# Activation sides in three stages, down slabs by column pairs, and state space copies on GpSimd's queue, in a decoder layer on one core

## The chip, the cores and the metric

The kernel runs on one core of a Trainium2 chip. A core has five engines, each with its own queue of instructions that it works off in order: TensorE (PE, matrix products), VectorE (DVE), ScalarE (ACT), GpSimd (POOL) and SyncE (SP, which here only starts transfers). They wait for each other by semaphores. Transfers between memory and SBUF are started by an instruction on some engine's queue and then run by themselves. The metric is the time of one execution on the device in microseconds (us), as the median of several runs.

## The reference

One decoder layer, for 512 tokens of width 1024, in float32:

```python
Layer = x + 1/2 SwiGLU(RMSNorm x)                       (macaron first half-step)
      -> x + W_out[ sig(g_nsa) * Y_nsa + sig(g_ssm) * Y_ssm ]   (parallel gated token mixers)
      -> x + 1/2 SwiGLU(RMSNorm x)                       (macaron second half-step)

def _rmsnorm(x, g):
    return xf * lax.rsqrt(jnp.mean(xf * xf, axis=-1, keepdims=True) + RMS_EPS) * g
def _swiglu(x, g, w_gate, w_up, w_down):
    h = _rmsnorm(x, g)
    return (jax.nn.silu(h @ w_gate) * (h @ w_up)) @ w_down
```

The hidden width of both feed-forward halves is 2816, which is 22 tiles of 128 (f tiles). Y_nsa is an attention with compressed, selected and windowed keys; Y_ssm is an S5 state space: u is projected from x, runs through a complex diagonal recurrence in time, gets a GELU and a gated linear unit.

## The kernel before, in words

Data lies transposed, features on the 128 partitions and the 512 tokens along the row. Every large product is made as three matmuls (`mm3`, L372): a float32 operand is split into a hi part (a copy rounded by ACT) and a lo part (the rest, by DVE), and hi x hi, lo x hi and hi x lo are added up in PSUM. Weights arrive as slabs of 128x1024 floats, which are eight blocks of 128x128. SP starts the transfers in the order of the plan (`wraw`, four buffers), ACT makes `whi` (L235), DVE `wlo` (L236), three buffers each, two slabs ahead of TensorE. A slab of eight blocks is 24 matmuls of 128x512.

TensorE's instructions stand in the order of the program; on the other engines a scheduler sets the order from the order of emission, priorities and dependencies, so what waits on an engine is also waited for by all that stands behind it there.

The second feed-forward half (`fast_ffn`, L481 on) has two parts. The first four f tiles are plain: gate and up, eight k blocks each. The other 18 are taken in nine pairs, gate and up of both tiles as a 2x2 block product by seven half-size products instead of eight (P1 to P7). Each product (`product`, L542) is 24 matmuls of 128x256. Their weight operands are sums of the four weight quarters, added up on DVE (L260) in `wpair` buffers (transfers of 512 KB) and then split like any slab. Their activation operands ("sides") are sums of the normalised x tiles k and k+4, in halves of 256 tokens: `side(k)` (L490) makes all seven for one k of four, on DVE, with hi copies `xqh` on ACT (L507) and `xql` on DVE (L508). `side(0)` to `side(2)` are emitted after plain tiles 1 to 3, the last one after tile 3 too. The results go to banks mA, mB and mC: P1, P6, P7 and P4 add up in mA, and ACT copies mA to SBUF after P1, P6 and P7 (`mP`, L563).

The down projection is added in five chunks (4 f tiles, then pairs 2, 2, 2, 3), as slabs of eight blocks that stand between products (`DOWN_AT`). A chunk's slabs can begin when its f tiles have their activation split into `ah` and `al` (L518, L519). `down` (L587) keeps one PSUM bank per output column that is begun; when a column has all f tiles of the chunk, DVE adds it to the residual (`xd`, read from `xhome`) and GpSimd's queue writes it back (L607), or in the last chunk SP stores the output.

The norm of the second half is made from `nacc` (sums of squares, GpSimd, L396); `norm.a` and `norm.b` (from L400) make the row factor `R` with small matmuls on TensorE.

In the state space part, `u_evac` (L977) writes a tile of u to DRAM and reads it back in another layout (one write of 256 KB, four reads of 64 KB); `s5_out` (L1081) does the same with the GELU's result in hi and lo halves: `gd` writes, `gT` reads. All of these are issued on the queue named `DU`, which is SP's. `s5m`, `str` and `sti` are the state's scratch tiles, `qh` and `ql` the query projection's parts, `kt` a transposed key.

Of the kernel before, what the change touches and what calls it, by code (L numbers as in the profile page):

```python
# [46 lines left out]

HEAD = 4
PAIR_CHUNKS = [2, 2, 2, 3]
DOWN_AT = [(1, 1), (1, 1), (1, 1), (1, 1), (1, 1), (1, 1), (1, 1), (1, 0), (1, 0)]  # L50


def fast_steps():

    np_ = (FF // 128 - HEAD) // 2
    ends = [HEAD]
    for n in PAIR_CHUNKS:
        ends.append(ends[-1] + 2 * n)
    down = []
    for c, e in enumerate(ends):  # L60
        b = ends[c - 1] if c else 0
        blocks = [(c, d, f) for d in range(KD) for f in range(b, e)]
        down.append([blocks[i:i + 8] for i in range(0, len(blocks), 8)])
    queue = []
    steps = [("plain", f) for f in range(HEAD)] + [("prod", 0, "P1")]
    nxt, done = 0, 0
    queue += down[0]
    for i in range(np_):
        a, b = DOWN_AT[i]
        steps += [("prod", i, "P2"), ("prod", i, "P6")]  # L70
        steps += [("down", queue.pop(0)) for _ in range(min(a, len(queue)))]
        steps += [("prod", i, "P5"), ("prod", i, "P7")]
        if i + 1 < np_:
            steps.append(("prod", i + 1, "P1"))
        steps += [("down", queue.pop(0)) for _ in range(min(b, len(queue)))]
        steps += [("prod", i, "P4"), ("prod", i, "P3")]
        done += 1
        if done == PAIR_CHUNKS[nxt]:
            assert not queue
            nxt, done = nxt + 1, 0  # L80
            queue += down[nxt]
    return steps + [("down", q) for q in queue], ends


# [210 lines left out]

def build(ctx, tc, xT_in, wstream, small_in, out):
    nc = tc.nc
    DU, DQ, DX = nc.sync, nc.sync, nc.sync
    V, S, G, PE = nc.vector, nc.scalar, nc.gpsimd, nc.tensor
    ctx.enter_context(tc.manual_schedule(engines={mybir.EngineType.PE}))  # L300
    cp = ctx.enter_context(tc.tile_pool(name="const", bufs=1))
# [5 lines left out]
    def H(name, dt=F32):  # L307
        return hp.tile([128, 512], dt, name=name, tag="h", bufs=NH)
# [25 lines left out]
    def smc(n, a=0, b=None):  # L334
        s, e = SM[n]
        return sm[:, s + a:(s + b if b is not None else e)]
# [144 lines left out]
    def fast_ffn(p, gname, x, norm, xgh, xgl, home, nxt):  # L481

        steps, ends = fast_steps()
        X = {}
        act, pss, left = {}, {}, {}
        bank, cq, ut = {}, {}, {}
        ng = cp.tile([128, KD], F32, name=f"ng_{p}")
        V.tensor_scalar(ng, smc(gname), -1.0, None, op0=ALU.mult)

        def side(k):  # L490

            R = norm.R
            a, b = slice(0, 256), slice(256, 512)
            ga, na, gb, nb = (t[:, i:i + 1] for i in (k, k + 4) for t in (smc(gname), ng))
            q1, q2, q3, q4 = (H(f"xq{i}") for i in range(4))
            V.scalar_tensor_tensor(q1[:, a], x[k][:, a], na, R[:, a], op0=ALU.mult, op1=ALU.mult)
            V.scalar_tensor_tensor(q4[:, b], x[k][:, b], ga, R[:, b], op0=ALU.mult, op1=ALU.mult)
            V.scalar_tensor_tensor(q2[:, a], x[k + 4][:, a], gb, R[:, a], op0=ALU.mult, op1=ALU.mult)
            V.scalar_tensor_tensor(q3[:, a], x[k + 4][:, b], nb, R[:, b], op0=ALU.mult, op1=ALU.mult)
            x[k] = x[k + 4] = None  # L500
            V.tensor_tensor(q1[:, b], q4[:, b], q1[:, a], op=ALU.add)
            V.tensor_tensor(q4[:, a], q4[:, b], q3[:, a], op=ALU.add)
            V.scalar_tensor_tensor(q3[:, b], q3[:, a], -1.0, q1[:, b], op0=ALU.mult, op1=ALU.subtract)
            V.tensor_tensor(q2[:, b], q2[:, a], q3[:, b], op=ALU.subtract)
            for q, nms in ((q1, ("P1", "P5")), (q2, ("P2", "P4")), (q3, ("P3", "P6"))):
                h, l = H("xqh", F32R), H("xql", F32R)
                S.activation(h, q, AF.Copy)  # L507
                V.tensor_tensor(l, q, h, op=ALU.subtract)  # L508
                for nm, c in zip(nms, (a, b)):
                    X[nm, k] = h[:, c], l[:, c]  # L510
            hl = H("xqhl", F32R)
            S.activation(hl[:, a], q4[:, a], AF.Copy)
            V.tensor_tensor(hl[:, b], q4[:, a], hl[:, a], op=ALU.subtract)
            X["P7", k] = hl[:, a], hl[:, b]

        def parts(f, u):
            ah, al = H("ah", F32R), H("al", F32R)
# [24 lines left out]
        def product(i, nm):  # L542
            bk = {"P1": "A", "P6": "A", "P7": "A", "P4": "A", "P2": "B", "P5": "C", "P3": "C"}[nm]
            first = nm in ("P1", "P2", "P5")
            if first:
                bank[i, bk] = PS(f"m{bk}")
            ps = bank[i, bk]
            hi, lo, _ = ws.slab("pair" if nm == "P1" else "prod")
            last = nm in ("P4", "P2", "P3")
            n = 0  # L550
            for u in range(2):
                o = ps[:, 256 * u:256 * u + 256]
                for k in range(4):
                    c = slice(u * 512 + k * 128, u * 512 + k * 128 + 128)
                    xh, xl = X[nm, k]
                    for w, xx in ((hi, xh), (lo, xh), (hi, xl)):
                        PE.matmul(o, w[:, c], xx, start=first and n == 0, stop=last and n == 23,  # L557
                                  skip_group_check=True)
                        n += 1
            f0 = HEAD + 2 * i  # L560
            if nm in ("P1", "P6", "P7"):
                t = H("m" + nm)
                S.activation(t, ps, AF.Copy)  # L563
                cq[i, nm] = t
            if nm == "P2":
                c = H("mc")
                V.tensor_tensor(c, ps, cq.pop((i, "P1")), op=ALU.subtract)
                del bank[i, bk]
                quarter(f0, 0, c)
            elif nm == "P7":  # L570
                c = H("mc")
                V.tensor_tensor(c, bank[i, "C"], cq.pop((i, "P7")), op=ALU.add)
                quarter(f0 + 1, 1, c)
            elif nm == "P4":
                c = H("mc")
                S.activation(c, ps, AF.Copy)
                del bank[i, bk]
                quarter(f0 + 1, 0, c)
                parts(f0 + 1, ut.pop(f0 + 1))
            elif nm == "P3":  # L580
                c = H("mc")
                V.scalar_tensor_tensor(c, ps, -1.0, cq.pop((i, "P6")), op0=ALU.mult, op1=ALU.subtract)
                del bank[i, bk]
                quarter(f0, 1, c)
                parts(f0, ut.pop(f0))
# [24 lines left out]
        for st in steps:  # L610
            if st[0] == "plain":
                f = st[1]
                ps = {nm: PS("gu") for nm in ("gate", "up")}
                for i, nm in enumerate(("gate", "up")):
                    for k in range(KD):
                        mm3(ps[nm], ws.blk(), xgh[k], xgl[k], k == 0, k == KD - 1)
                    if i == 0 and held:
                        norm.b()
                        plain_end(0, held)
                        held = None  # L620
                if f == 0:
                    norm.a()
                    held = ps
                    ws.fetch(p, 0)
                else:
                    plain_end(f, ps)
                    side(f - 1)
                ps = None
                if f == HEAD - 1:
                    for k in range(KD):  # L630
                        xgh[k] = xgl[k] = None
                    for k in range(HEAD - 1, 4):
                        side(k)
# [1013 lines left out]
```

## Time and profile before

| | |
|---|---|
| median of 3 runs | 1173.25 us (1171.51 to 1174.67) |
| profiled execution, span | 1173.91 us, 1172.2 us |
| busy: TensorE, DVE, ACT, GpSimd | 1128.1, 807.1, 465.0, 229.2 us |
| share of the span | 96%, 69%, 40%, 20% |
| mean clock granted to TensorE | 0.981 of full speed |

The profile is one execution. A row of an engine's waits says who released the wait, by semaphores, and for how long the engine stood idle. The chain is followed back from the last instruction. A window adds up an engine's busy time in a stretch; beside it stands PEclk, the clock that TensorE was granted there as a share of full speed. A matmul's own duration in a group overlaps its neighbours (it is pipelined), so the pitch between starts is what it costs; the chain's pieces are such pitches.

### The profile page before, as it was taken

Reading aid. Unit: us, or ns where it says so; the run is one execution under the profiler, and the core shown is the slowest. Engines: PE = TensorE matmul, PEld = TensorE weight load, DVE = VectorE, ACT = ScalarE, POOL = GpSimd, SP = SyncE. Lnnn points to the kernel's source line nnn. Section 1 sums busy time; section 2 is a strip of 40 time slices with the busy share of each in tenths; the row PEclk is TensorE's granted clock in tenths of the full one; section 3 lists DMA queues with packets and bytes.
Section 4 is the critical chain, followed back from the end, with each engine's and each line's share of the span. In section 5 each row is a group of like instructions: output and inputs, shape, how many; then the busy total and the mean of one; then the engine's idle time right before and its main releaser. Section 6 shows DMA issues by size and latency. Waiting matters only on the chain.

```text
span 1172.2 us, 16105 instructions
## 1 busy us (share of the span) xinstructions
PE 1128.1 (96%) x6061; PEld 968.2 (83%) x6061; DVE 807.1 (69%) x1504; ACT 465.0 (40%) x748; POOL 229.2 (20%) x400
## 2 busy tenths in 40 slices
PE   9999999999999999799999999999499999999988
PEld 6888888888888898688788888888399898988977
DVE  6996554556547477789899866556957677776852
ACT  6321323232225112546666643343244444443530
POOL 2039530128425064200000000130000000000000
PEclk9999999999999999799999999999799999999999
DMA  7223232222234433561111122652234345454231
GB/s 278 89 92 108 90 95 86 90 90 90 93 106 162 149 112 104 168 197 55 55 55 55 54 72 91 205 207 90 72 119 165 134 165 182 171 179 145 84 132 72
DMA packets 51646, 139.44 MB, mean 119 GB/s; under 512 B 6256, under 2 KB 12656, under 8 KB 51568
## 3 DMA queue, kind: packets, MB, share of 16 engines
q1 hardware_dynamic: 48224, 127.79, 33.3%
q0 software_dynamic: 3200, 10.49, 2.3%
q8 instruction: 47, 0.77, 0.3%
q14 instruction: 31, 0.25, 0.1%
q10 hardware_dynamic: 144, 0.13, 0.0%
HBM read 118.47 MB, written 17.83 MB: 116 GB/s over the span
## 4 chain that ended last, share of the span: by engine, by line
PE 77%; issue 8%; DVE 7%; DMA 4%; ACT 2%; POOL 1%; SPq 0%; ACTq 0%; DVEq 0%; POOLq 0%
PE gu L375 8%; PE gu L376 8%; PE gu L374 8%; PE mA L557 7%; PE dn L376 6%; PE dn L374 6%; PE dn L375 6%; PE mC L557 4%; DMA wpair<-wstream 3%; PE mB L557 2%; DMA wraw<-wstream 1%; DVE wlo L236 1%; PE wo L375 1%; PE wo L374 1%; PE wo L376 1%
## 5 line engine op out<-in xcount | busy, mean ns | idle before, releaser
L235 ACT ACTIVATE whi<-wraw 128x1024 fp32r<-128x1024 f32 (+2 forms) x149 | 155.7, 1045 | 381.4 <-issue 107.1
L236 DVE TENSOR_TENSOR wlo<-wraw,whi 128x1024 fp32r<-128x1024 f32 (+2 forms) x149 | 187.4, 1258 | 74.2 <-ACT whi L235 70.5
L374 PE MATMUL gu<-xgh,whi 128*128 128x512 f32 x416 | 163.5, 393 | 0.5 <-ACT xgh L381 0.5
L375 PE MATMUL gu<-xgh,wlo 128*128 128x512 f32 x416 | 162.1, 390 | 0.4 <-DVE wlo L236 0.4
L374 PE MATMUL dn<-ah,whi 128*128 128x512 f32 x352 | 140.1, 398 | 7.8 <-ACT ah L518 7.8
L376 PE MATMUL dn<-al,whi 128*128 128x512 f32 x352 | 139.2, 396 | 0.7 <-DVE al L519 0.7
L375 PE MATMUL dn<-ah,wlo 128*128 128x512 f32 x352 | 139.3, 396 | 0.0
L376 PE MATMUL gu<-xgl,whi 128*128 128x512 f32 x352 | 137.3, 390 | 0.1
L228 DVE TENSOR_TENSOR wlo<-wpair,whi 128x1024 fp32r<-128x1024 f32 x63 | 77.0, 1223 | 28.5 <-ACT whi L227 28.2
L227 ACT ACTIVATE whi<-wpair 128x1024 fp32r<-128x1024 f32 x63 | 66.5, 1056 | 72.9 <-issue 42.4
L374 PEld LDWEIGHTS gu<-xgh,whi 128*128 128x128 f32 x416 | 78.2, 188 | 17.3 <-ACT xgh L381 1.0
L375 PEld LDWEIGHTS gu<-xgh,wlo 128*128 128x128 f32 x416 | 78.2, 188 | 17.2 <-DVE wlo L236 0.8
L374 PEld LDWEIGHTS dn<-ah,whi 128*128 128x128 f32 x352 | 67.3, 191 | 22.8 <-ACT ah L518 9.5
L376 PEld LDWEIGHTS dn<-al,whi 128*128 128x128 f32 x352 | 67.3, 191 | 16.8 <-DVE al L519 2.6
L607 POOL DMA_DIRECT2D xhome<-xd x32 | 17.3, 540 | 317.6 <-DVE xd L606 305.9
L557 PE MATMUL mA<-xqh,whi 128*128 128x256 f32 x216 | 62.5, 289 | 16.5 <-ACT xqh L507 15.8
L375 PEld LDWEIGHTS dn<-ah,wlo 128*128 128x128 f32 x352 | 67.4, 191 | 13.2
L376 PEld LDWEIGHTS gu<-xgl,whi 128*128 128x128 f32 x352 | 66.1, 188 | 14.2 <-DVE xgl L382 0.5
L557 PE MATMUL mA<-xql,whi 128*128 128x256 f32 x216 | 62.4, 289 | 1.6 <-DVE xql L508 1.6
L557 PE MATMUL mA<-xqh,wlo 128*128 128x256 f32 x216 | 62.2, 288 | 0.0
L557 PEld LDWEIGHTS mA<-xqh,whi 128*128 128x128 f32 x216 | 42.2, 195 | 17.5 <-ACT xqh L507 16.3
L1427 ACT ACTIVATE P<-P,aw,qs 128x128 f32<-128x128 f32 (+1 forms) x64 | 41.6, 650 | 31.8 <-DVE aw L1426 31.7
(452 smaller groups left out, 2667.6 us busy)
## 6 DMA issues: line engine op xcount, KB each, us to landing
wraw<-wstream SPq DMA_DIRECT2D x151, 512.0 KB, 3.5
wpair<-wstream SPq DMA_DIRECT2D x36, 512.0 KB, 6.0
xd<-xhome SPq DMA_DIRECT2D x40, 256.0 KB, 4.5
xhome<-xd POOLq DMA_DIRECT2D x32, 256.0 KB, 3.6
x<-xT SPq DMA_DIRECT2D x8, 256.0 KB, 5.1
xspill<-x SPq DMA_DIRECT2D x8, 256.0 KB, 2.2
gT<-gd SPq DMA_DIRECT2D x32, 64.0 KB, 2.0
x<-xspill SPq DMA_DIRECT2D x8, 256.0 KB, 4.9
```

The costliest lines, as they stand in the source:

```text
L227: nc.scalar.activation(hi, src, AF.Copy)
L228: nc.vector.tensor_tensor(lo, src, hi, op=ALU.subtract)
L235: nc.scalar.activation(hi[:, c], raw[:, c], AF.Copy)
L236: nc.vector.tensor_tensor(lo[:, c], raw[:, c], hi[:, c], op=ALU.subtract)
L374: PE.matmul(ps, hi, xh, start=start, stop=False)
L375: PE.matmul(ps, lo, xh, start=False, stop=False)
L376: PE.matmul(ps, hi, xl, start=False, stop=stop)
L557: PE.matmul(o, w[:, c], xx, start=first and n == 0, stop=last and n == 23, skip_group_check=True)
L607: nc.gpsimd.dma_start(home[d], xd)
L1427: S.activation(p[:, :n], p[:, :n], AF.Exp, bias=w[:, 1:2], scale=qc, accum_out=w[:, 2:3])
```

## The change

Four things are changed.

1. `DU`, the queue of the state space copies, is GpSimd's instead of SP's: 4 writes and 16 reads for u, 8 writes and 32 reads for the GELU's result.
2. `side(k)` is replaced by three stages, each over all four k. `side1` (P1, P2 and P3) multiplies x by R on GpSimd, scales by the norm's gain on ACT and splits on ACT and DVE; `side2` (P5, P6) and `side3` (P7, P4) combine these tiles. The signs that the operands had are put into the evacuations of the banks. `norm.a` is emitted after the gate of plain tile 0, and `norm.b`, the end of tile 0 and `side1` after two k blocks of the gate of tile 1, `side2` after tile 2, `side3` after tile 3.
3. The order of products and down slabs is written out as strings: before any pair a down slab, P1 of the first pair, and a second down slab; then per pair such as `26D57ND43` (a digit is the pair's product, N the next pair's P1, D a down slab).
4. A down slab holds four columns of two f tiles (the column half outermost, then f pairs), not the f tiles of one column after the other.

```diff
-DOWN_AT = [(1, 1), (1, 1), (1, 1), (1, 1), (1, 1), (1, 1), (1, 1), (1, 0), (1, 0)]
+LEAD = "D1D"
+SEQ = ["265D7N43", "26D57N43"] + ["26D57ND43"] * 4 + ["26D57ND43", "26D57N43", "2657D43"]
...
-        blocks = [(c, d, f) for d in range(KD) for f in range(b, e)]
-        down.append([blocks[i:i + 8] for i in range(0, len(blocks), 8)])
+        down.append([[(c, d, f) for f in (g, g + 1) for d in range(h, h + 4)]
+                     for h in range(0, KD, 4) for g in range(b, e, 2)])
...
-    DU, DQ, DX = nc.sync, nc.sync, nc.sync
+    DU, DQ, DX = nc.gpsimd, nc.sync, nc.sync
...
+        def cut(q, k, nms):
+            h, l = H("xqh", F32R), H("xql", F32R)
+            S.activation(h, q, AF.Copy)
+            V.tensor_tensor(l, q, h, op=ALU.subtract)
...
+        def side1():
+            for k in range(4):
+                for j in (k, k + 4):
+                    xn[j] = H("xn")
+                    G.tensor_tensor(xn[j], x[j], norm.R, op=ALU.mult)
+                    x[j] = None
+                    S.activation(xn[j], xn[j], AF.Copy, scale=smc(gname, j, j + 1))
+                hl = H("xqhl", F32R)
+                S.activation(hl[:, a], xn[k][:, a], AF.Copy)
+                V.tensor_tensor(hl[:, b], xn[k][:, a], hl[:, a], op=ALU.subtract)
+                X["P1", k] = hl[:, a], hl[:, b]
+                cut(xn[k + 4], k, ("P2", "P3"))
...
+        def side2():
+            for k in range(4):
+                q = tt[k] = H("xt")
+                V.tensor_tensor(q[:, a], xn[k][:, a], xn[k][:, b], op=ALU.subtract)
+                V.scalar_tensor_tensor(q[:, b], q[:, a], -1.0, xn[k + 4][:, b], op0=ALU.mult, op1=ALU.subtract)
+                cut(q, k, ("P5", "P6"))
...
+        def side3():
+            for k in range(4):
+                q = H("xt")
+                G.tensor_tensor(q[:, a], xn[k + 4][:, b], xn[k][:, b], op=ALU.subtract)
+                V.scalar_tensor_tensor(q[:, b], tt.pop(k)[:, b], -1.0, xn[k + 4][:, a],
+                                       op0=ALU.mult, op1=ALU.subtract)
+                xn[k] = xn[k + 4] = None
+                cut(q, k, ("P7", "P4"))
...
-                V.tensor_tensor(c, ps, cq.pop((i, "P1")), op=ALU.subtract)
+                V.tensor_tensor(c, ps, cq.pop((i, "P1")), op=ALU.add)
...
-                    if i == 0 and held:
-                        norm.b()
-                        plain_end(0, held)
-                        held = None
+                        if held and k == 1:
+                            norm.b()
+                            plain_end(0, held)
+                            held = None
+                            side1()
+                    if f == 0 and nm == "gate":
+                        norm.a()
```

Where the instructions stand now is shown at three places. The first is SP's queue in the state space part, around the copies of the GELU's result of its first finished tile (gd to DRAM, gT back); wraw is a weight slab, qh and ql are copies for the query heads. Before:

```order
L208 DMA wraw_3997<-wstream 128x1024
L1096 DMA gd10_3254<-gh_3980 128x512
L1096 DMA gd11_3255<-gl_3981 128x512
L208 DMA wraw_4038<-wstream 128x1024
L1100 DMA gT_3985<-gd10_3254 32x4x128 x4
L1100 DMA gT_3991<-gd11_3255 32x4x128 x4
L1278 DMA qh_4025<-qh_4025 64x512
L1278 DMA ql_4026<-ql_4026 64x512
L1278 DMA qh_4031<-qh_4031 64x512
L1278 DMA ql_4032<-ql_4032 64x512
L208 DMA wraw_4052<-wstream 128x1024
```

And now:

```order
L206 DMA wraw_3997<-wstream 128x1024
L206 DMA wraw_4038<-wstream 128x1024
L206 DMA wraw_4052<-wstream 128x1024
L206 DMA wraw_4145<-wstream 128x1024
L1293 DMA qh_4025<-qh_4025 64x512
L1293 DMA ql_4026<-ql_4026 64x512
L1293 DMA qh_4031<-qh_4031 64x512
L1293 DMA ql_4032<-ql_4032 64x512
L206 DMA wraw_4200<-wstream 128x1024
```

The ten copies are gone from SP, and the two slabs that stood behind them follow the slab before them. The second place is GpSimd in the same part, where the last combinations of one state tile (str, sti) are followed by the subtractions for the next (s5m). Before:

```order
L1075 TENSOR_TENSOR str_3893<-s5m0_3869,s5m2_3871 128x4x127
L1076 TENSOR_TENSOR sti_3894<-s5m4_3887,s5m5_3888 128x4x127
L1055 TENSOR_TENSOR s5m0_4079<-s5m0_4079,s5m1_4080 128x512
L1056 TENSOR_TENSOR s5m2_4081<-s5m2_4081,s5m3_4082 128x512
L1074 MEMSET str_4103 128x4
L1074 MEMSET sti_4104 128x4
L1075 TENSOR_TENSOR str_4103<-s5m0_4079,s5m2_4081 128x4x127
L1076 TENSOR_TENSOR sti_4104<-s5m4_4097,s5m5_4098 128x4x127
```

And now:

```order
L1090 TENSOR_TENSOR str_3893<-s5m0_3869,s5m2_3871 128x4x127
L1091 TENSOR_TENSOR sti_3894<-s5m4_3887,s5m5_3888 128x4x127
L1111 DMA gd10_3254<-gh_3980 128x512
L1111 DMA gd11_3255<-gl_3981 128x512
L1115 DMA gT_3985<-gd10_3254 32x4x128 x4
L1115 DMA gT_3991<-gd11_3255 32x4x128 x4
L1070 TENSOR_TENSOR s5m0_4079<-s5m0_4079,s5m1_4080 128x512
L1071 TENSOR_TENSOR s5m2_4081<-s5m2_4081,s5m3_4082 128x512
L1089 MEMSET str_4103 128x4
L1089 MEMSET sti_4104 128x4
L1090 TENSOR_TENSOR str_4103<-s5m0_4079,s5m2_4081 128x4x127
L1091 TENSOR_TENSOR sti_4104<-s5m4_4097,s5m5_4098 128x4x127
```

Between the two tiles stand the ten copies of the finished output. The third place is ACT at the first pair's products: mP1 and mP6 are the copies of bank mA after P1 and P6, whi a weight slab's hi part, xqh a side's hi part. Before:

```order
L507 ACTIVATE xqh_7574<-xq0_7562 128x512
L507 ACTIVATE xqh_7578<-xq1_7563 128x512
L507 ACTIVATE xqh_7582<-xq2_7564 128x512
L512 ACTIVATE xqhl_7586<-xq3_7565 128x256
L563 ACTIVATE mP1_7620<-mA_7589 128x512
L235 ACTIVATE whi_7623<-wraw_7463 128x1024
L227 ACTIVATE whi_7658<-wpair_7242 128x1024
L538 ACTIVATE th_7654<-mc_7651 128x256
L563 ACTIVATE mP6_7688<-mA_7589 128x512
```

And now:

```order
L225 ACTIVATE whi_7701<-wpair_7240 128x1024
L492 ACTIVATE xqh_7565<-xt_7562 128x512
L233 ACTIVATE whi_7736<-wraw_7626 128x1024
L492 ACTIVATE xqh_7572<-xt_7569 128x512
L492 ACTIVATE xqh_7579<-xt_7576 128x512
L576 ACTIVATE mP1_7652<-mA_7615 128x512
L551 ACTIVATE th_7732<-mc_7729 128x256
L225 ACTIVATE whi_7767<-wpair_7237 128x1024
L576 ACTIVATE mP6_7764<-mA_7615 128x512
```

The copy after P1 stood behind the last sides of the stage and ahead of all the later splits; now it stands behind the hi parts of P5's weights and of a down slab (`whi_7736`) and three parts of the third stage.

## Rows read from the trace of the kernel before

**Rows 1.** Page, section 1, TensorE: busy us, share, instructions

```profile
PE 1128.1 (96%) x6061; PEld 968.2 (83%) x6061; DVE 807.1 (69%) x1504; ACT 465.0 (40%) x748; POOL 229.2 (20%) x400
```

**Rows 2.** Waits of TensorE, whole span: total us, times, longest us

```profile
PE mA L557 <- ACT xqh L507: 15.8, 2, 11.1
PE dn L374 <- ACT ah L518: 7.8, 4, 2.9
PE kt L1183 <- DVE ql L1276: 6.1, 1, 6.1
PE s5y L1087 <- DVE ge L965: 1.8, 1, 1.8
```

**Rows 3.** Chain that ended last, 826:860 us: start us, us, what

```profile
828.70 0.24 PE gu L376
...
839.38 0.69 DVE al L519
...
848.67 3.87 PE mA L557 x15
...
856.16 2.88 PE mA L557 x24
```

**Rows 4.** DVE in a stretch: us, busy (count), PEclk, DMA share, GB/s

```profile
812.00:852.00 40.00, 36.75 (x67) 0.77 0.23 78
```

**Rows 5.** DVE groups, 830:860 us: busy us, mean ns, idle before

```profile
L508 DVE TENSOR_TENSOR xql<-xq,xqh 128x512 fp32r<-128x512 f32 x9 | 6.0, 690 | 1.4 <-ACT xqh L507 1.4
...
L236 DVE TENSOR_TENSOR wlo<-wraw,whi 128x1024 fp32r<-128x1024 f32 x1 | 1.2, 1225 | 2.1 <-ACT whi L235 2.1
L496 DVE SCALAR_TENSOR_TENSOR xq<-x,ng_ffn,R 128x256 f32<-128x256 f32 x2 | 1.0, 479 | 0.0
```

**Rows 6.** ACT groups, 826:860 us, columns as in Rows 5

```profile
L507 ACT ACTIVATE xqh<-xq 128x512 fp32r<-128x512 f32 x9 | 5.3, 625 | 11.4 <-DVE xq L501 8.8 <-DVE xq L504 2.7
...
L563 ACT ACTIVATE mP<-mA 128x512 f32<-128x512 f32 x2 | 1.2, 598 | 3.0 <-PE mA L557 3.0
L235 ACT ACTIVATE whi<-wraw 128x1024 fp32r<-128x1024 f32 x1 | 1.0, 1047 | 0.0
```

**Rows 7.** TensorE at the four chunk ends, columns as in Rows 4

```profile
920.00:932.00 12.00, 9.95 (x46) 0.86 0.33 111
988.00:996.00 8.00, 6.31 (x30) 1.00 0.28 106
1052.00:1060.00 8.00, 6.13 (x20) 0.79 0.32 122
1132.00:1144.00 12.00, 9.10 (x32) 0.86 0.70 238
```

**Rows 8.** DMA issues, stores of the result: count, KB each, median us to landing

```profile
outT<-xd SPq DMA_DIRECT2D x8, 256.0 KB, 2.0
```

**Rows 9.** SP's queue, 455 to 476 us: start us, us, instruction

```profile
462.97 0.33 SPq L1096 DMA_DIRECT2D gd<-gh  x1
...
464.12 0.39 SPq L208 DMA_DIRECT2D wraw<-wstream  x1
465.04 3.89 SPq L1100 DMA_DIRECT2D gT<-gd  x8
```

**Rows 10.** ACT, 466 to 476 us, as Rows 9, idle before in brackets

```profile
468.63 1.06 ACT L235 ACTIVATE whi<-wraw 128x1024 fp32r<-128x1024 f32 x1 [5.69 <-DMA wraw<-wstream]
```

**Rows 11.** POOL, 470 to 488 us, columns as in Rows 10

```profile
474.81 1.27 POOL L1055 TENSOR_TENSOR s5m<-s5m,s5m 128x512 f32<-128x512 f32 x1 [15.96 <-DVE s5m L1052]
```

**Rows 12.** POOL groups, whole span, columns as in Rows 5

```profile
L396 POOL TENSOR_TENSOR nacc<-nacc,nsq 128x512 f32<-128x512 f32 x14 | 22.9, 1637 | 17.8 <-ACT nsq L395 17.8
L607 POOL DMA_DIRECT2D xhome<-xd x32 | 17.3, 540 | 317.6 <-DVE xd L606 305.9 <-DMA xd<-xhome 11.2 <-issue 0.2
```

**Rows 13.** POOL busy in a stretch, columns as in Rows 4

```profile
455.00:540.00 85.00, 11.47 (x8) 0.92 0.52 155
```

**Rows 14.** TensorE, first product that reads gT, columns as in Rows 9

```profile
536.76 0.39 PE L374 MATMUL fg<-gT,whi 128*128 128x512 f32 x1
```

More of the change, by code (lines that the diff above doesn't have):

```diff
@@ L49 @@
 PAIR_CHUNKS = [2, 2, 2, 3]
-DOWN_AT = [(1, 1), (1, 1), (1, 1), (1, 1), (1, 1), (1, 1), (1, 1), (1, 0), (1, 0)]
+LEAD = "D1D"
+SEQ = ["265D7N43", "26D57N43"] + ["26D57ND43"] * 4 + ["26D57ND43", "26D57N43", "2657D43"]
 def fast_steps():
-    np_ = (FF // 128 - HEAD) // 2
     ends = [HEAD]
@@ L61, in fast_steps @@
         b = ends[c - 1] if c else 0
-        blocks = [(c, d, f) for d in range(KD) for f in range(b, e)]
-        down.append([blocks[i:i + 8] for i in range(0, len(blocks), 8)])
[L64 to L81, printed above, removed]
+        down.append([[(c, d, f) for f in (g, g + 1) for d in range(h, h + 4)]
+                     for h in range(0, KD, 4) for g in range(b, e, 2)])
+    steps = [("plain", f) for f in range(HEAD)]
+    queue = down.pop(0)
+    left = list(PAIR_CHUNKS)
+    for i, seq in enumerate([LEAD] + SEQ):
+        for ch in seq:
+            if ch == "D":
+                steps.append(("down", queue.pop(0)))
+            else:
+                steps.append(("prod", i if ch == "N" else max(i - 1, 0), "P1" if ch == "N" else "P" + ch))
+        if i:
+            left[0] -= 1
+            if left[0] == 0:
+                assert not queue
+                left.pop(0)
+                queue = down.pop(0)
     return steps + [("down", q) for q in queue], ends
@@ L486, in fast_ffn @@
         bank, cq, ut = {}, {}, {}
[L487 to L514, printed above, removed]
@@ new lines, in fast_ffn @@
+        a, b = slice(0, 256), slice(256, 512)
+        xn = [None] * KD
+        tt = {}
+        def cut(q, k, nms):
+            h, l = H("xqh", F32R), H("xql", F32R)
+            S.activation(h, q, AF.Copy)
+            V.tensor_tensor(l, q, h, op=ALU.subtract)
+            for nm, c in zip(nms, (a, b)):
+                X[nm, k] = h[:, c], l[:, c]
+        def side1():
[10 more added lines that the diff above has]
+                cut(xn[k + 4], k, ("P2", "P3"))
@@ L571, in product @@
                 c = H("mc")
-                V.tensor_tensor(c, bank[i, "C"], cq.pop((i, "P7")), op=ALU.add)
+                V.scalar_tensor_tensor(c, bank[i, "C"], -1.0, cq.pop((i, "P7")), op0=ALU.mult, op1=ALU.subtract)
                 quarter(f0 + 1, 1, c)
@@ L575, in product @@
                 c = H("mc")
-                S.activation(c, ps, AF.Copy)
+                S.activation(c, ps, AF.Copy, scale=-1.0)
                 del bank[i, bk]
@@ L581, in product @@
                 c = H("mc")
-                V.scalar_tensor_tensor(c, ps, -1.0, cq.pop((i, "P6")), op0=ALU.mult, op1=ALU.subtract)
+                V.tensor_tensor(c, ps, cq.pop((i, "P6")), op=ALU.add)
                 del bank[i, bk]
@@ L613, in fast_ffn @@
                 ps = {nm: PS("gu") for nm in ("gate", "up")}
-                for i, nm in enumerate(("gate", "up")):
+                for nm in ("gate", "up"):
                     for k in range(KD):
                         mm3(ps[nm], ws.blk(), xgh[k], xgl[k], k == 0, k == KD - 1)
-                    if i == 0 and held:
-                        norm.b()
-                        plain_end(0, held)
-                        held = None
+                        if held and k == 1:
[5 more added lines that the diff above has]
+                        norm.a()
                 if f == 0:
-                    norm.a()
                     held = ps
@@ L626, in fast_ffn @@
                     plain_end(f, ps)
-                    side(f - 1)
                 ps = None
-                if f == HEAD - 1:
+                if f == HEAD - 2:
+                    side2()
+                elif f == HEAD - 1:
                     for k in range(KD):
                         xgh[k] = xgl[k] = None
-                    for k in range(HEAD - 1, 4):
-                        side(k)
+                    side3()
                     norm.R = None
```

## The prediction

> **What bounds the kernel now.** I read the page first, then the waits of TensorE, then its busy time in windows, then the chain that ended last in the windows that had holes. The page says that TensorE is busy 1128.1 us of the 1172.2 us span, 96% [rows 1]. So what can be won is the time in which it waits, and the time in which it runs below full clock after a wait; the same 6061 matmuls are issued by both kernels. The list of TensorE's waits names four places that the change touches [rows 2]: the first product of the second feed-forward waits 15.8 us in two pieces for `xqh` (the hi half of an activation side, from ACT); the down projection waits four times, 7.8 us in all, for `ah` (the hi half of the gated activation); a transpose of the mixing stage waits 6.1 us for a query's `ql`; and the third state space output waits 1.8 us for `ge` (the GELU's scratch).
>
> The chain shows what the first wait really costs. The last plain matmul ends at 828.70 + 0.24 = 828.94, and P2, the second product, ends at 856.16 [rows 3]. One product is 24 matmuls in 2.88 us at full clock [rows 3], so two of them need 5.76 us and took 27.22: **21.5 us are lost there**, of which the wait for `xqh` is only a part; the rest is the wait for `xql`, and matmuls at a low clock (15 matmuls of 128x256 took 3.87 us, which is 0.26 each instead of 0.12, the lower of the clock's two levels, after TensorE had stood still). Who is late? DVE was busy 36.75 of the 40 us from 812 to 852 [rows 4], with the sides and the ends of the plain tiles. So this stage is bound by DVE, with ACT between two DVE steps.
>
> The four chunk ends are read from windows [rows 7]. In each I add the idle time and busy x (1 - clock): 2.05 + 9.95 x 0.14 = 3.4; 1.69 + 0 = 1.7; 1.87 + 6.13 x 0.21 = 3.2; 2.90 + 9.10 x 0.14 = 4.2. Together 12.4 us, of which the list of waits shows 7.8. In three of the four the clock costs about 1.3 us on top of the idle time.
>
> **The change part by part.** The sum is made against the profiled execution, 1173.9 us (span 1172.2 and 1.7 around it), which is 0.7 above the median of 1173.25.
>
> *Sides in three stages.* Removed from DVE per k: four scalar_tensor_tensor that scale x (0.48 us each [rows 5]) and part of the additions; GpSimd now multiplies eight x tiles by R, ACT scales them, and DVE keeps per k about one xql for each of three stages (0.69 [rows 5]), one xqhl and the combinations. The new time for the first stage: the norm's R is now made two k blocks into the second plain tile. Three plain tiles of 48 matmuls of 128x512 (0.24 each, twice the 0.12) last 3 x 11.5 = 34.6 us by this and end at 828.94, so R is there at about 828.94 - 34.6 + 1.4 + 1 = 797. GpSimd then needs 8 x 1.64 = 13.1 us, by the nearest row of the same shape, `nacc` [rows 12], and is done near 810, ACT and DVE a few us later, with whole plain tiles as cover. Between 797 and the start of P1 lie 32 us plus the down slab that now stands first (24 x 0.24 = 5.8); GpSimd would have to be 2.5 times as slow as this row before P1 waited. So the 21.5 us go: **-21.5**. What is late next? The down slab after P1 needs the activations of plain tile 3, whose last part, `al`, was ready at 839.38 + 0.69 = 840.1 [rows 3]. In the new order TensorE comes to it at 828.9 + 5.8 (first slab) + 2.9 (P1) + 2.9 (half a slab on tile 2) = 840.5, with DVE's queue about as full: I take **+1** (0 to 3).
>
> *A new wait at P6.* P6 adds into the bank that P1 wrote, so it waits until ACT has copied P1's result away (`mP1`). The order of ACT now puts this copy behind the hi split of the next down slab, which reuses P2's weight buffer and so can't start before P2's last matmul, and behind two xqh; the second of these needs a DVE operand that stands behind that slab's lo split. From P2's end that is whi 1.05, wlo 1.22, xql 0.69, one combination 0.48, xqh 0.63, copy 0.60 [rows 5, 6] = **+4.7**, and about +1.3 for the clock after a wait of this length (the chunk ends above): together +6.0 (0 to 9: 0 if the split finds its buffer sooner than I read the order). Behind the waiting split stand the copy and the next splits of ACT; TensorE is the one that waits for them.
>
> *Down slabs by columns.* Before, a column's eight blocks ran through all of the chunk's f tiles, so the first slab needed the chunk's newest activations. Now the first slab takes the chunk's oldest pair and four columns. The wait of the last pair's `ah` has at least one slab and three products before it: **-12.4** (half of it, if something else is late there, -6). The four columns of each half end together, so that at the kernel's end four evacuations and four stores of 256 KB leave close together instead of spread: a store lands in 2.0 us [rows 8], and three more behind it: **+1** (0 to 3).
>
> *State space copies on GpSimd's queue.* Removed from SP: 60 issues. In before SP issues `gd` at 462.97, waits for it, and the weight slab of the next query projection leaves at 464.12, with eight gT behind it until 468.9 [rows 9]. ACT stood 5.69 us for that slab, until 468.63 [rows 10], and `ql` and the 6.1 us wait hang on it. Now SP has only weights there, so the slab can leave earlier, at most those 5.69 us. But GpSimd must now issue two gd and eight gT before it gets to the two subtractions of the next state space tile, which began at 474.81 [rows 11]. At the 0.54 us of its own 32 copies to DRAM [rows 12] the issues end at 462.97 + 1.1 + some 2.5 for gd to land + 4.3 = 471, so they begin up to 4 us sooner; at 1 us each it is 475, no sooner. The third state space output hangs on that. Between the ends 0 and -5.7, I take **-2**: the wait moves from the transposes to `s5y`. If GpSimd's issue costs more than 1 us this part turns positive. The u copies (20 issues, 11 us of GpSimd by that price) stand before any reader by far: 0 (0 to +2).
>
> **The sum:** -21.5 + 1 + 6.0 - 12.4 + 1 - 2 = -27.9. 1173.9 - 27.9 = 1146.0, or 1145 against the median. I forecast **1145**.
>
> **A rule weighed against the trace.** The row for GpSimd's copies shows 540 ns each, 32 of them beside a DVE that was busy 69% of the span [rows 12, 1], and nothing that looks like a held issue. The Trainium skill says on its page "SBUF — State Buffer", section "A bandwidth-pool intuition that's wrong (but worth ruling out)", that a DMA issued by GpSimd needs a port that a DVE instruction may hold, and gives about 620 ns alone and about 3100 ns beside one. By that figure 40 gd and gT issues would be an estimated 124 us, and the kernel near 1208; by the row they are 22 us. The row speaks against the rule here, but it is from another stage, with other DVE instructions, so the rule gets a rival of its own below.
>
> **The rivals.**
> 1. *DVE and ACT stay the bound at the start of the products.* The work is moved, not cut, and 92% busy from 812 to 852 [rows 4] speaks for it; against it: four of 0.48 us per k leave DVE, and stages two and three are needed only products later. If half of the 21.5 us stays: 1145 + 10.8 = **1156**.
> 2. *No wait at P6*, because ACT's copy gets by in time: 1145 - 6 = **1139**. For it: a wait read from an order alone is never sure; against: the buffer's reuse is plain in that order.
> 3. *GpSimd's queue becomes the bound of the state space* (slower). The place is gd and gT of the four outputs: 40 issues between 462.97 and the first matmul that reads gT at 536.76 [rows 9, 14], 73.8 us, of which GpSimd's own 11.5 us of work [rows 13] go off: 62.3 us, or 1.56 us each, are hidden. If each issue is held by two running 1.22 us DVE instructions [rows 5], it costs 0.54 + 2.44 = 2.98 us, together 119.2, 57 over the cover: 1145 + 2 + 57 = **1204**. It decides from 1.56 us, and the kernel is slower than before from about 2.2 us (26 us more over 40 issues). Against it stand the 540 ns.
> 4. *The change does not do what it says* at the chunk ends: another operand of the slabs is late there. Half of 12.4 stays: **1151**.
>
> **How the numbers follow.** Chances: forecast (1140 to 1150) 0.47, rival 1 0.17, rival 2 0.16, rival 4 0.10, rival 3 0.06; the last 0.04 is some gain lost that I don't see, near no change. The range from 1135 to 1159 holds the forecast and rivals 1, 2 and 4 with their spread, and leaves out rival 3 and most of the last. A difference of 0.3% (3.5 us) is what can be told from none here: faster needs a time under 1169.7. Rivals 1, 2, 4 and the forecast are all on that side, 0.90, and 0.01 of the rest: faster 0.91, same 0.03, slower 0.06.
>
> **What would show it right or wrong.** Right: no wait of P1 for xqh or xql; one of 4 to 5 us before P6's first matmul, released by ACT's `mP`; no `dn` waiting for `ah` at 920, 990, 1055, 1135 (shifted by what was won before); `kt` waiting 3 us or less and `s5y` more than 1.8 us; gT issues of 0.5 to 0.6 us on GpSimd. Wrong: DVE full and TensorE standing between the last plain tile and P5; gT issues beyond 1.5 us or `fg` waiting for gT; waits of the plain tiles for `wlo` because DVE has stage one in its queue.

## The result, and the profile after

The changed kernel takes 1155.91 us (median of 4 runs, 1154.71 to 1157.60; before in the same rounds 1173.18); the ratio is 0.9854, 95% interval 0.9836 to 0.9873. I had forecast 1145 with a range from 1135 to 1159: faster, as forecast, and inside the range, but by 17 us where I had worked out 28. The profiled execution has a span of 1153.8 us against 1172.2, 18.4 less.

The busy line of the page, which answers to [rows 1], says that TensorE's work is nearly the same and that GpSimd has 50 us more:

```profile
PE 1124.5 (97%) x6061; PEld 967.4 (84%) x6061; DVE 807.1 (70%) x1483; ACT 469.3 (41%) x756; POOL 279.7 (24%) x472
```

To see where the 18.4 us come from I cut the span at two instructions that both kernels have: the first and last starts of the down projection's first matmuls (`dn<-ah,whi`) and of the plain tiles' `gu<-xglb,whi`. They are found in the groups of one tile's instructions (count, duration ns min/median/max, first and last start in us). For the kernel before, and then for the changed one:

```profile
L376 PE MATMUL gu<-xglb,whi x64: 388/389/397, 783.8 to 828.5; 128*128 128x512 f32 x64
...
L374 PE MATMUL dn<-ah,whi x352: 388/390/760, 73.5 to 1167.6; 128*128 128x512 f32 x176
```

```profile
L374 PE MATMUL gu<-xglb,whi x64: 389/389/398, 788.3 to 833.0; 128*128 128x512 f32 x64
...
L372 PE MATMUL dn<-ah,whi x352: 389/389/628, 74.2 to 1149.0; 128*128 128x512 f32 x176
```

| stretch, us | before | after | change |
|---|---|---|---|
| up to the first down matmul of the first feed-forward half | 73.5 | 74.2 | +0.7 |
| from there to the first matmul of the plain tiles ("mixing") | 710.3 | 714.1 | +3.8 |
| the plain tiles (first to last start) | 44.7 | 44.7 | 0 |
| last plain to last down matmul ("products") | 339.1 | 316.0 | -23.1 |
| from there to the end of the span | 4.6 | 4.8 | +0.2 |

So the products gave 23.1 us, and the mixing stage, of which I had expected -2, took 3.8 back. TensorE's waits after the change (engine, what it waited for, total us, times, longest us), to be held against [rows 2]:

```profile
PE mA L570 <- ACT mP L576: 6.6, 2, 4.6
PE s5y L1103 <- POOL str L1090: 4.1, 1, 4.1
PE kt L1198 <- DVE ge L980: 3.6, 1, 3.6
PE dn L372 <- ACT ah L531: 3.2, 1, 3.2
```

The waits for `xqh` and for the chunk ends are gone. New are `mP` (4.6 of the 6.6 us at P6, 2.0 at the last pair), `str` and one long `ah`. The chunk ends lay at 920, 988, 1052 and 1132 [rows 7], and the same slabs start at 917, 979, 1041 and 1117 in the new kernel. The windows of 25 us from 900 (busy, count, granted clock, DMA share, GB/s) are all full there up to 1100; the one after it lacks the 2.0 us of the last pair and no more. The four with these slabs:

```profile
900.00:925.00 25.00, 25.00 (x190) 1.00 0.43 148
...
975.00:1000.00 25.00, 25.00 (x168) 1.00 0.38 124
...
1025.00:1050.00 25.00, 25.00 (x170) 1.00 0.56 190
...
1100.00:1125.00 25.00, 23.02 (x139) 1.00 0.62 220
```

At the start of the products the chain (start us, us, what) shows both new waits in a row:

```profile
848.03 0.69 DVE al L532
...
848.76 0.79 PE dn L374
849.55 0.43 PE dn L372
...
852.78 1.69 PE mB L570 x15
...
855.73 1.06 ACT whi L233
...
856.81 1.23 DVE wlo L234
858.04 0.60 DVE xql L493
858.64 0.35 DVE xt L524
...
859.07 0.07 ACT xqh L492
...
859.61 0.59 ACT mP L576
...
860.24 5.46 PE mA L570 x24
```

TensorE waits for the activation of plain tile 3, 3.2 us for `ah` and then 0.3 us for `al`, until 848.76, and then runs matmuls of 128x512 at 0.43 us instead of 0.23. DVE's timeline (start us, us, instruction, idle before in brackets) shows why it is late: the second stage's last `xql` stands ahead of tile 3's first step, `g`, whose gate TensorE had made by 828:

```profile
841.61 0.69 DVE L493 TENSOR_TENSOR xql<-xt,xqh 128x512 fp32r<-128x512 f32 x1 [0.70 <-ACT xqh L492]
842.22 0.68 DVE L537 TENSOR_TENSOR g<-gu,R 128x512 f32<-128x512 f32 x1
```

P2 ends at 855.66 (852.78 + 2.88). Then comes the row that I had read off the order: the down slab's hi split on ACT, its lo split on DVE, xql, the combination xt, xqh, and at last the copy mP; P6 begins at 860.24, 4.58 us after P2, and takes 5.46 instead of 2.88 us at the lower clock level (columns as in the windows above):

```profile
860.00:864.00 4.00, 3.76 (x17) 0.50 0.86 307
```

From the last plain matmul's end (833.44) to P6's end (865.70) TensorE needs 32.3 us for two slabs of 5.47 and three products of 2.88, 19.6 us at full clock: 12.7 us are still lost there, of the 21.5 before.

In the mixing stage GpSimd's timeline (start us, us, instruction, idle before in brackets) shows what happened to the u copies. After:

```profile
417.72 2.18 POOL L1000 DMA_DIRECT2D up<-ud  x4 [4.48 <-DMA ud<-u]
419.91 2.56 POOL L1039 TENSOR_TENSOR bq<-kce,sm 128x496 f32<-128x496 f32 x2
422.44 1.26 POOL L1070 TENSOR_TENSOR s5m<-s5m,s5m 128x512 f32<-128x512 f32 x1
...
449.23 3.38 POOL L1090 TENSOR_TENSOR str<-s5m,s5m 128x508 f32<-128x508 f32 x1 [3.67 <-DVE s5m L1082]
...
474.32 4.36 POOL L1115 DMA_DIRECT2D gT<-gd  x8 [4.17 <-issue]
```

And before, the instructions that answer to the second, the third and the fourth row of these:

```profile
411.44 2.58 POOL L1024 TENSOR_TENSOR bq<-kce,sm 128x496 f32<-128x496 f32 x2 [28.90 <-DVE kce L1016]
416.41 1.30 POOL L1055 TENSOR_TENSOR s5m<-s5m,s5m 128x512 f32<-128x512 f32 x1 [2.39 <-DVE s5m L1052]
...
443.55 3.41 POOL L1075 TENSOR_TENSOR str<-s5m,s5m 128x508 f32<-128x508 f32 x1 [3.68 <-DVE s5m L1067]
```

The four `up` reads of a tile stand on GpSimd until the write of u has landed: 4.48 us in the row shown, 2.5, 4.2 and 2.9 us for the other three tiles. GpSimd gets to `bq` and to the first state tile's subtraction at 422.44 instead of 416.41, and `str` starts 5.7 us later, at 449.23 instead of 443.55. TensorE waits 4.1 us for it. The eight gT issues take 4.36 us, 0.55 each.

### The profile page after: what moved, and what is told of

Read it like the earlier page. It is cut to its first block, busy times and chain, and to the rows that moved or that the text cites. A ratio compares the mean times of both kernels' runs of the same rounds, so it can differ in the third digit from the quotient of the medians.

```text
span 1153.8 us, 16163 instructions
## 1 busy us (share of the span) xinstructions
PE 1124.5 (97%) x6061; PEld 967.4 (84%) x6061; DVE 807.1 (70%) x1483; ACT 469.3 (41%) x756; POOL 279.7 (24%) x472
## 5 line engine op out<-in xcount | busy, mean ns | idle before, releaser
L226 DVE TENSOR_TENSOR wlo<-wpair,whi 128x1024 fp32r<-128x1024 f32 x63 | 76.9, 1220 | 23.1 <-ACT whi L225 23.1
L373 PEld LDWEIGHTS dn<-ah,wlo 128*128 128x128 f32 x352 | 66.4, 189 | 13.1
```

Of the source, the lines that this page charges most:

```text
L226: nc.vector.tensor_tensor(lo, src, hi, op=ALU.subtract)
L373: PE.matmul(ps, lo, xh, start=False, stop=False)
```

## The experiments

In the table, mixing and products are the stretches of the table above, read from each run's trace; the times are medians, each beside a kernel before of 1172.9 to 1174.1.

| run | time | ratio, 95% | mixing | products |
|---|---|---|---|---|
| before | 1173.2 | | 710.3 | 339.1 |
| after | 1155.9 | 0.9854 (0.9836 to 0.9873) | 714.1 | 316.0 |
| e1 copies on SP | 1151.9 | 0.9805 (0.9786 to 0.9825) | 708.1 | 316.3 |
| e2 u on SP, GELU on GpSimd | 1152.3 | 0.9809 (0.9790 to 0.9829) | 708.7 | 316.5 |
| e3 before, copies on GpSimd | 1177.7 | 1.0035 (1.0017 to 1.0053) | 714.7 | 340.0 |
| e4 third stage after P1 | 1154.9 | 0.9831 (0.9813 to 0.9849) | 716.6 | 313.7 |
| e5 old slabs after chunk 0 | 1170.2 | 0.9970 (0.9952 to 0.9988) | 715.8 | 326.1 |
| e6 slabs between products | 1154.4 | 0.9834 (0.9809 to 0.9859) | 709.2 | 318.1 |
| e7 stages two, three later | 1147.0 | 0.9767 (0.9747 to 0.9787) | 709.7 | 311.8 |
| e8 e7 and a slab behind P2 | 1147.8 | 0.9770 (0.9748 to 0.9792) | 709.9 | 312.8 |
| e9 third stage after P2 | 1147.2 | 0.9778 (0.9762 to 0.9794) | 708.6 | 311.6 |
| e10 third stage after P6 | 1146.8 | 0.9768 (0.9751 to 0.9784) | 710.1 | 312.0 |
| e11 old sides, new order | 1153.6 | 0.9826 (0.9811 to 0.9840) | 708.6 | 318.4 |
| e12 e10, xql on GpSimd | 1146.7 | 0.9770 (0.9751 to 0.9789) | 709.3 | 311.3 |

**The queue of the copies: e1, e2, e3.** Three kernels with the queue alone changed.

```diff
-    DU, DQ, DX = nc.gpsimd, nc.sync, nc.sync
+    DU, DQ, DX = nc.sync, nc.sync, nc.sync          # e1; e3 the other way, in before
...
-        DU.dma_start(ud[t], u)                      # e2, and the same for the up reads
+        nc.sync.dma_start(ud[t], u)
```

> The changed kernel with all 60 state space copies back on SP's queue. Theory A: putting the copies on GpSimd's queue cost the mixing stage the 3.8 us that the two profiles show between the first down projection and the last matmul before the second feed-forward half, so 1155.9 - 3.8 = 1152, with the 6.1 us wait of kt back and no wait of s5y for str. Rival B: that stretch differs from execution to execution, or the later shift comes from elsewhere; then 1155 to 1157.

> The changed kernel with only the u copies (4 writes, 16 reads) back on SP; the GELU's gd and gT stay on GpSimd. Theory A1: the u reads, each standing on GpSimd until u's write has landed, held back the state tiles (first s5m subtraction 422.4 instead of 416.4); without them it is at 416 to 417 again, s5y no longer waits for str, and the GELU copies alone keep the small gain that I forecast (0 to 4 us): 1148 to 1152, not slower than all copies on SP. Rival A2: the GELU copies on GpSimd are what costs: about 1155, s5m of the last tiles still near 478.

> The kernel before with nothing changed but the queue of the 60 copies (GpSimd's). Theory A: 3.8 us slower than before, 1177, with s5y waiting about 4 us for str. Rival: as before within 1.5 us, 1173 (the cost needs the other parts of the change).

Theory A was right in e1 and e3, 1151.9 and 1177.7 us, and A1 in e2, 1152.3 us, as to the u copies, though not as to the small gain. The mixing stretch tells the two groups apart without overlap. With the u copies on SP (ten kernels: before, e1, e2, e6 to e12) it is 708.1 to 710.3 us, with them on GpSimd (after, e3, e4, e5) 714.1 to 716.6, so the means lie 6.1 us apart. The rival that the GELU's copies cost it is out: e2 leaves them on GpSimd and has 708.7. But they don't give anything either: e2 is not faster than e1. The waits of e1, and then of e2:

```profile
PE kt L1198 <- DVE ql L1291: 5.8, 1, 5.8
...
PE kt L1198 <- DVE ge L980: 0.9, 1, 0.9
PE s5y L1102 <- DVE ge L980: 0.9, 1, 0.9
```

```profile
PE kt L1198 <- DVE ge L980: 4.2, 1, 4.2
PE s5y L1102 <- DVE ge L980: 3.2, 1, 3.2
```

In e1 `kt` waits 5.8 and 0.9 us, then `s5y` 0.9; in e2 `kt` 4.2 and `s5y` 3.2. The sums, 7.6 and 7.4 us, are the same: the wait moved from the transposes to the output, as I had said, but none of it was won. In e3 the 3.8 us wait for `str` is there in the kernel before too:

```profile
PE s5y L1088 <- POOL str L1075: 3.8, 1, 3.8
```

**The down slabs: e5.**

```diff
+        blocks = [(c, d, f) for d in range(KD) for f in range(b, e)]
+        if c == 0:
+            blocks = [(c, d, f) for h in range(0, KD, 4) for g in range(b, e, 2)
+                      for f in (g, g + 1) for d in range(h, h + 4)]
+        down.append([blocks[i:i + 8] for i in range(0, len(blocks), 8)])
```

> The changed kernel, but from the second chunk on a down slab again takes all f tiles of one column (the first chunk keeps the column pairs). Theory E: the four chunk-end waits went because the first slab of a chunk no longer needs the newest pair; they come back, 12.4 us in idle time and clock: 1166 to 1169, dn waiting for ah four times, 7 to 8 us in all. Rival F: they went because of the new order of products and slabs; then 1155 to 1158.

Theory E, a little over its range: the products take 326.1 us instead of 316.0, and the median is 14 us above the changed kernel's (its runs spread from 1164.9 to 1173.2, and the profiled one was at their lower end). TensorE's waits have the chunk ends again, 8.3 us in five waits for `ah`, of which one, 3.2 us, is that of the second down slab, which the changed kernel has as well; the other four, 5.1 us, stand for the 7.8 us before:

```profile
PE dn L375 <- ACT ah L534: 8.3, 5, 3.2
PE mA L573 <- ACT mP L579: 6.6, 2, 4.6
```

**The wait of P6: e4, e6.** Two ways to take the copy `mP` out of the row of ACT.

```diff
-                    side3()                         # e4: out of the end of plain tile 3
...
                 product(*st[1:])
+                if st[1:] == (0, "P1"):
+                    side3()
```

> The changed kernel with the third stage of sides emitted after P1 instead of before the first down slab, so that ACT's copy of bank mA after P1 stands ahead of that stage's xqh and of the down slab's split. Theory C: the wait of P6 for mP (4.6 us and about 2.9 us more in 5.46 instead of 2.87 us... of P6 at the low clock, 1.3 to 2.6) goes: 5.5 to 7 us less, 1149 to 1150. Rival D: the time returns as a wait of P7 or of the down slab before it, because the third stage is now late: 1153 to 1156.

P6's wait went and P6 ran in 2.88 us, but the products took only 2.3 us less (313.7), and the time, 1154.9, is rival D's: the next slab, the one after P5, now waits. Its chain:

```profile
862.47 1.69 PE mC L570 x15
...
865.43 1.07 ACT whi L225
...
866.52 1.23 DVE wlo L226
867.75 0.61 DVE xd L619
...
868.41 0.50 PE dn L372
```

The slab's banks are freed by DVE (`xd`), and that instruction stands behind a lo split, whose hi split begins when P5 ends (862.47 + 2.88 = 865.35).

```diff
-LEAD = "D1D"
-SEQ = ["265D7N43",
+LEAD = "1"                                          # e6, with the copies on SP
+SEQ = ["2D6D57ND43",
```

> The changed kernel with the copies on SP and another order at the start: P1 and P2 at once after the plain tiles, then down slab, P6, down slab, P5 (LEAD 1, first string 2D6D57ND43). The same matmuls. Without it (copies on SP) 1151.9, and 316.8 us from the last plain matmul to the last down matmul. Theory C: the waits of the second slab for ah (3.5 us and about 2 of clock) and of P6 for mP (4.6 and about 2.5) are only a matter of what stands before them; both go: 305 to 308 us, 1140 to 1143. Rival D: DVE and ACT are full there, so the same time comes back as waits for sides or weight parts: 313 to 317, 1148 to 1152.

Both theories were too hopeful. The products took 318.1 us, 1.8 more than in e1: P6 waits 13.1 us for `mP`, since the copy still stands behind all of the third stage's xqh and P6 now comes earlier:

```profile
PE mA L570 <- ACT mP L576: 15.1, 2, 13.1
```

So a slab between P2 and P6 does not help as long as ACT's order is kept; what stands ahead of the copy on ACT decides.

**The stages of the sides: e7 to e10, e12.** With the copies on SP, the second stage emitted after the end of plain tile 3, and the third after P1 (e7), with a slab moved behind P2 as well (e8), after P2 (e9) or after P6 (e10).

```diff
-                if f == HEAD - 2:
-                    side2()
-                elif f == HEAD - 1:
+                if f == HEAD - 1:
                     for k in range(KD):
                         xgh[k] = xgl[k] = None
-                    side3()
+                    side2()
...
+                if st[1:] == (0, "P1"):             # e9: "P2", e10: "P6"
+                    side3()
```

> The changed kernel with the copies on SP, the order of products kept, but the second stage of sides emitted after the end of plain tile 3 (it was before) and the third after P1. Theory G: al of tile 3 was late because it stands on DVE behind the second stage; now it is ready by 836 and the slab after P1 does not wait (minus 5.6), nor does P6 for mP (minus 4.6 and clock, but in the run with the third stage later alone a wait of the slab after P5 for a bank came in its place, 2.4 us): 308 to 311 us for the stage, 1143 to 1146. Rival D: P6 then waits for its own sides, which DVE now makes 4 to 6 us later: 314 to 317, 1149 to 1152.

> Copies on SP, sides later as in the run before, and the second down slab moved behind P2 (LEAD D1, first string 2D65D7N43). Theory C with G: no wait before P5 at all: 304 to 307 us for the stage, 1139 to 1142, the same as the order with slabs between the products. Rival D: 313 to 317, 1148 to 1152.

In e7 the slab after P1 no longer waits for `ah` and `al`, nor P6 for `mP`: 311.8 us, 4.5 less than e1, and 1147.0 in all. Theory G was right on both waits and a little too hopeful on the rest, since the wait of e4 is longer here, 5.1 us for `mc`, the sum of bank mB, behind the third stage on DVE:

```profile
848.35 1.69 PE mC L570 x15
...
856.30 0.61 DVE mc L580
857.05 0.77 PE dn L372
```

e8 has the same 5.1 us and 312.8, and 1147.8 in all: far from theory C with G, and just under rival D's ranges.

> Copies on SP, second stage of sides after plain tile 3, third stage after P2 (in the run before, after P1: 1147.0, with a new wait of 5.1 us of the third down slab for mc, which stood on DVE behind the third stage). Theory J: with mc ahead of the third stage on DVE that slab gets its banks in time, and the third stage has P6, P5 and the slab (11 us) before P7: the 5.1 us and about 2.5 of clock go, 304 to 307 us for the stage, 1139 to 1142. Rival D: P7 waits for its sides instead: 309 to 313, 1144 to 1148.

In e9 `mc` comes early and that slab doesn't wait, but P7 does, 6.0 us for `mP`, now the copy after P6, which stands on ACT behind the third stage's last xqh: rival D, though by the copy and not the sides.

```profile
860.34 0.35 DVE xt L524
...
861.31 0.59 ACT mP L576
...
861.94 11.00 PE mA L570 x72
```

> As the run before, third stage after P6. Theory J: as that run within 1 us as long as P7's sides are there at the end of the slab, or 1 to 3 us more if the one product that the stage is later is waited for. Rival: 1144 or more.

e10 has the copy after P6 ahead of the third stage. Now P7 waits for the sides themselves, piece by piece, and the time is the same again. The list shows only 2.8 us, but TensorE was busy only 0.82 us in each of the windows 858 to 860 and 860 to 862, and the granted clock is 0.50 from 862 to 868:

```profile
PE mA L570 <- ACT xqh L492: 1.8, 3, 0.7
...
PE mA L570 <- DVE xql L493: 1.0, 2, 0.5
```

> The run with the third stage after P6 (1146.8; its remaining waits at the start are some 3 us before P7 for the third stage's xqh and xql, with about 2.5 of clock), with two edits: the four xql of the third stage go from DVE (0.69 each) to GpSimd (1.3 each by the same shape there), and a down slab of pair 6 moves to pair 8, behind its P6, where P6 waited 2.0 us for mP. Theory L: the start is now bound by how much DVE has to do between P2 and P7; with 2.8 us less on DVE most of P7's wait goes, and the 2.0 us too: 306 to 310 us for the stage, 1141 to 1144. Rival M: GpSimd's subtractions become what P7 waits for (8 of them in a row, some 8 us): 311 to 314, 1145 to 1148.

```diff
-SEQ = [..., "26D57ND43", "26D57N43", "2657D43"]
+SEQ = [..., "26D57N43", "26D57N43", "26D57D43"]
...
-            V.tensor_tensor(l, q, h, op=ALU.subtract)
+            E.tensor_tensor(l, q, h, op=ALU.subtract)    # G in the third stage
```

The 2.0 us of the last pair went (no wait for `mP` is left), and the third stage became GpSimd's own row, some 3 us per k, in which each xql waits for ACT's xqh, and each xqh for the xt before it:

```profile
856.00 0.91 POOL L523 TENSOR_TENSOR xt<-xn 128x256 f32<-128x256 f32 x1
857.65 1.46 POOL L493 TENSOR_TENSOR xql<-xt,xqh 128x512 fp32r<-128x512 f32 x1 [0.74 <-ACT xqh L492]
```

GpSimd begins this row only at 851.9, behind four stores of `xhome` that waited for DVE's `xd` until 849.0. Rival M: P7 waits 3.3 us for xqh and 2.4 for GpSimd's xql, twice what it waited in e10; with the 2.0 us won at the last pair the products come to 311.3.

**Order or sides: e11.** The kernel before with `fast_steps` of the changed one, nothing else.

> The kernel before (sides made per k on DVE, copies on SP, old places of the norm) with the new order of products and the new down slabs. Theory H: the new order alone takes the four chunk ends (12.4 us), and the first slab fills half of the stand at P1: the last xqh comes 20 us after the last plain matmul, so of the 21.5 us at the start some 12 stay (as a wait of P1 or of its sides), and P6 has no wait: 317 to 321 us from the last plain matmul to the last down matmul (before 339.6, changed kernel with copies on SP 316.8), 1151 to 1156. Rival K: the three stages are what matters: the start is lost whole, 326 or more, 1160 or more.

Theory H: 318.4 us and 1153.6. The waits at the start are shorter than before, 9.4 instead of 15.8 us for `xqh`:

```profile
PE mA L555 <- ACT xqh L505: 9.4, 2, 5.6
```

So of the 22.8 us between before and e1, 20.7 come from the order and the slabs, and the three stages, placed as the change places them, add 2.1, one profile each. Placed later (e7 to e10, and e12), with the slab moves of e8 and e12, they add 5.6 to 7.1.

## Why the prediction was right in direction and short in size

**The chunk ends (-12.4).** Right, and somewhat more: the products without any wait are 22 slabs of 5.47 and 63 products of 2.88 (their length at full clock in both traces), 301.8 us. Before lost 37.8 us on top of that (339.6 from the end of the last plain matmul to the end of the last down matmul), 21.5 at the start and so 16.3 after it, where my windows summed 12.4 and I left out the wait of 0.7 for `mP`. By the starts of the matmuls the four ends lost 15.1: a record is 0.39 us long at a pitch of 0.23, so the idle time between records, which the windows count, misses some tenths at each wait. The changed kernel loses 2.0 after the start. The gain there is 14.3 us; e5 gives 10.1 of it back by the slabs alone. Rival 4 is out.

**The start (-21.5, then +1 and +6.0).** The old waits went as said, but the -21.5 stood under the three stages, and e11 shows that they are not what most of the gain came from: with the old sides and the new order 14.6 us are lost at the start (318.4 less the 301.8 and the 2.0 of the last pair), with the stages as well 12.7. The step that failed is "I take +1 (0 to 3)" for the second slab's wait for `al`. I had set DVE's queue "about as full" as before and thus kept 840.1 as the time; but the second stage, which is emitted before the end of tile 3, stands ahead of it on DVE, and `al` was ready at 848.7. Two slabs and two products took 22.2 us instead of 16.7: 5.5, and not 1. e7, which turns round these two and puts the third stage later, takes it away. P6's wait was right to a tenth (4.58 for 4.7), with the place and the releaser that were read off the order; the clock after it cost 2.58 and not 1.3, since the whole of P6 ran at the lower level. Together 12.7 us for 7.0.

**The state space copies (-2).** Two steps failed. The u copies, which I set at "0 (0 to +2)" because no reader was near, cost 4 to 6 us: 4.0 in the median between the changed kernel and e1, 3.6 to e2, a ratio of 1.0035 in e3, and 4.4 to 6.0 in the mixing stretch of these pairs. I looked for who reads `up` on TensorE and not for what stands behind the reads on GpSimd, its own `bq` and `s5m`. By the rows the larger part is not the issue, 0.55 us each, but the wait of a tile's reads for the landing of u's write, 2.5 to 4.5 us, on a queue that then has computing to do; on SP the same order cost TensorE nothing that shows. No run takes the wait apart from the issues (2.2 us for the last four reads). The GELU's copies, set at -2, give nothing (e1 against e2).

**GpSimd's issue.** The row of the changed kernel, 4.36 us for eight gT, is 0.55 us each, as the xhome row had it [rows 12]; rival 3 is out, and no first matmul that reads gT waited. The Trainium skill's page "SBUF — State Buffer", section "A bandwidth-pool intuition that's wrong (but worth ruling out)", with some 3100 ns for such a transfer beside a DVE copy, does not show here in the issue. What did lengthen is the landing: the median of the gT reads is 5.0 us on GpSimd's queue, 2.0 before on SP's; whether DVE has a part in that, no run here tells.

**The end (+1), and the sum.** The end of the kernel took 0.2 us more, so the stores were set too high. The profile's -18.4 is -8.8 at the start, -14.3 at the chunk ends, +0.2 at the end, +3.8 in the mixing stage and +0.7 before it, which I did not follow up; the forecast of -27.9 had -14.5, -12.4, +1, -2 and 0.

**Rivals 1 and 2.** Rival 2 (no wait at P6) is out. Rival 1, the start still bound by DVE and ACT, is in its substance what happened, not by half of the old waits but by two new ones. e4, e7 to e10 and e12 show the same thing further on: each order takes away one wait and leaves 2.4 to 6.0 us at the next instruction that stands behind the third stage (the slab's bank, P7's copy, P7's sides). Whether that floor, some 10 us over the 301.8, is DVE's amount of work or only the order on the three engines stays open; e12 took 2.8 us from DVE and did not tell, since GpSimd's row, late by its own queue, took its place.

**A better version.** e7, e9, e10 and e12 lie within 0.6 us of each other at 1146.7 to 1147.2 us, some 9 us under the changed kernel and 26 under the one before: the change's order, slabs and stages, with stages two and three later and the copies on SP.

## What to carry to other kernels

Before a transfer that waits for an earlier one's landing is issued on an engine that computes, look at what stands behind it there: that pays for the wait as well as for the issue. The u copies cost 4 to 6 us in this way; the GELU's copies, whose reads waited there too (1.9 and 2.5 us for the first two tiles in e2), cost nothing, since a wait only moved. When work is emitted earlier to be ready in time, look at what it now stands ahead of, on every engine that it uses: here both new waits at the start were evacuations behind sides that were not yet due. And read the order of the engines between two instructions that are to follow each other: the one wait that I took from it came out to a tenth of a microsecond; the ones that I estimated from "about as full" did not.

## What was not expected of the hardware

The gT reads on GpSimd's queue land later than on SP's, 5.0 against 2.0 us in the median for 64 KB (4.5 in e2 and 5.4 in e3 on GpSimd's, 2.1 in e1 on SP's). And after 4.58 us without a matmul all 24 matmuls of P6 ran at the lower level of the clock, 1.2 GHz (5.46 us for 2.88; the granted clock is 0.50 from 860 to 864): 2.6 us on top of the wait, where before idle times of 1.9 to 2.9 us cost about 1.3 [rows 7]. The 2.0 us before the last pair's P6 cost nothing on top (1.00 from 1100 to 1125), so the length of the wait alone does not tell what the clock will cost.
